# The passage from the out projection to the gate: the first products' copies placed by priority, T3's differences before the weights' sums, the norm's sums and spread behind one more product

## The chip, the cores and the metric

The kernel runs on one core of a Trainium2 chip. Its engines are TensorE (PE, with its weight loads PEld), VectorE (DVE), ScalarE (ACT), GpSimd (POOL) and SyncE (SP, which issues the DMAs). The metric is device time in microseconds; lower is better. The kernel before takes 1813.62 us, the median of three runs from 1813.46 to 1816.01.

## The reference

One layer of a hybrid decoder on 1024 tokens (and 16 meta tokens) of width 1024:

```python
h = h + jnp.concatenate([o_sb, o_ssm, o_mla], axis=-1) @ w_out[i].astype(dt)

fn = rmsnorm(h, ffn_norm_g[i])
h = h + (jax.nn.silu(fn @ w_gate[i].astype(dt)) * (fn @ w_up[i].astype(dt))) @ w_down[i].astype(dt)
```

`rmsnorm` divides each token by the root of its mean square and multiplies by a gain per channel. The three mixers (stick-breaking attention, SSD, MLA) come before, and a last norm behind. D_FF is 2816, that is 22 units of 128.

## The kernel before, in words

Everything is held with channels on the partitions: `hT[f]` is the f-th 128 channels by 1024 tokens, in two halves of 512 tokens (`HALF[c]`, c = 0 and 1). All matrix products are made in three matmuls: an operand is split into a high part (a cast, on ScalarE) and a low part (value less high part, on POOL or DVE), and high x high, low x high and high x low are summed in PSUM. `split` (L1076) is that pair: L1077 the cast, L1078 the subtraction.

The passage in question starts with the last quarter of the out projection. `last_rows(f, c)` (L1171) makes 12 matmuls (L1177 to L1179) for channel block f and half c and adds them to `hT[f]` on DVE (L1084). Half c = 0 goes into the banks named `d_ps`, half c = 1 into those named `b_ps`. When a half is complete, `squares` (L1186) stores it to DRAM, squares it on ScalarE (L1190) and adds the squares in two groups. `row_sums` (L153 on PE, L164 on DVE, the power on POOL L165; the tile is `rc`) makes each token's reciprocal root, and `row_spread` (L171 on PE) spreads it over the 128 partitions of a bank `row`. `normed` (L1117, DVE) multiplies by gain and row.

The gate and up products are made by a seven-product scheme (Strassen's) on 2 x 2 blocks: units 2p and 2p + 1 of the weights by halves of channels, against halves of channels by halves of tokens. `u11` and `u21` are the normed half c = 0 of channels 0 to 3 and 4 to 7; their split tiles are called B11 and B21 (tiles `raw`). The second half's operands are T1, T2, T3, T4 and B22, differences and sums of normed blocks. T3 is made from hT before the norm is known: ScalarE scales `hT[i]` by the gain (L1372), DVE multiplies `hT[4 + i]` by its gain and subtracts (L1374), and when the second row is there DVE multiplies the result by it (L1388). T2 = T3 + u11 (L1084) is then split into its hi and lo.

`GateUp(p)` holds one pair of units. `load` brings the weights, `sums` (L1268) makes the weights' differences and sums on DVE (four for gate, four for up; L1081 and L1084, tiles `raw` and `s2`), `split_sums` splits them. `top_first` is the first product, with B11, into two banks A (gate, up) and copies A to `r` on ScalarE (L1316); `top_second` adds the second product, with B21, to the same banks, and so can't start in a bank before it is copied. Pair p = 1 (`second`) loads its first weights early (`load_early`) and makes its `top` right behind that of p = 0; its `r` is the tile `grow`. `rest` makes the other five products; DVE adds them up (L1084, tiles `u`), with sigmoid on ScalarE (L1302) and two products on DVE (L1303, L1304). The pairs from p = 2 on follow in a loop.

What sets the order: each engine works its instructions off in the order in which they stand in its queue. A planner with a model of the engines' times places instructions where it expects them to be ready; program order is the start, `tc.high_priority(offset=n)` lets an instruction compete as if it stood n places earlier, and `tc.issue_after(ins)` keeps an instruction behind `ins` on that instruction's engine. `last_on(engine)` is the last instruction written for an engine so far.

## Time and profile before

| | us |
|---|---|
| median of 3 runs | 1813.62 |
| the profiled execution | 1819.26 |
| its span, first to last instruction | 1817.3 |
| PE busy in the span | 1722.8 (95%) |
| DVE busy | 1214.3 (67%) |
| ACT busy, POOL busy | 860.0, 858.4 (47% each) |

The last rows of the out projection run from 1055 us on, the first gate products from 1108, and the third pair of units is reached at about 1200. In a row of the timeline stand start, duration, engine, line, operation, out<-in and shape, the number of merged instructions (x4), and in brackets how long the engine was idle before and what ended that. In a row of the busy time by stretch stand the stretch, its length, the busy time of each engine with the number of instructions, the granted TensorE clock (1.00 is full), the DMA engines' share and GB/s. In the chain of waits stand start, time and engine with the tile.

### The profile page before, as it was taken

To read this page: it belongs to the slowest core of one execution; us is meant where nothing else is said; L and a number is where in the kernel's file an instruction comes from. 1 tells how busy PE (TensorE), PEld (TensorE's weight loads), DVE (VectorE), ACT (ScalarE), POOL (GpSimd) and SP (SyncE) were. 2 spreads that over 40 slices of the span, in tenths; PEclk is the share of its full clock that TensorE was granted. 3 is DMA by queue.
4 is the path that set the end of the run, shared out by engine and by line. 5 is a ranking of instruction groups with operands and counts; after the bars stand their busy time and mean duration, and the time that the engine had idled before them with its cause. 6 is when DMAs were issued, how large, how long until landed. Compare 5 with 4: busy or idle time off the path is not lost.

```text
span 1817.3 us, 26447 instructions
## 1 busy us (share of the span) xinstructions
PE 1722.8 (95%) x9769; PEld 1506.0 (83%) x9769; DVE 1214.3 (67%) x1801; ACT 860.0 (47%) x1878; POOL 858.4 (47%) x597
## 2 busy tenths in 40 slices
PE   7969999999999999999999998999999999799997
PEld 7859998999987778998888876778888888677787
DVE  8686655777544673455576558967776667899854
ACT  7545564555566646775544424422232223334333
POOL 4433334343366557563321345634333234678783
PEclk9969999999998999999999998999999999899999
DMA  4211232222443546347221342232222233733102
GB/s 157 60 53 44 78 88 73 64 70 66 116 148 106 187 159 171 103 124 263 78 88 53 108 140 102 64 99 83 80 76 81 71 98 140 286 100 95 47 1 93
DMA packets 121012, 186.93 MB, mean 103 GB/s; under 512 B 21986, under 2 KB 81412, under 8 KB 120884
## 3 DMA queue, kind: packets, MB, share of 16 engines
q1 hardware_dynamic: 101488, 169.69, 29.6%
q10 hardware_dynamic: 19396, 15.56, 2.8%
q8 instruction: 77, 1.26, 0.3%
q14 instruction: 51, 0.42, 0.1%
HBM read 131.61 MB, written 53.60 MB: 102 GB/s over the span
## 4 chain that ended last, share of the span: by engine, by line
PE 68%; DVE 17%; ACT 4%; issue 3%; DMA 3%; POOL 3%; SPq 1%; ACTq 0%; DVEq 0%; POOLq 0%
PE d_ps L142 8%; PE d_ps L143 8%; PE d_ps L144 8%; PE b_ps L1295 7%; PE b_ps L1297 7%; PE b_ps L1296 7%; DVE raw L1081 2%; PE ptg L317 2%; PE b_ps L1498 1%; PE b_ps L1497 1%; PE ptg L319 1%; PE pv L295 1%; PE b_ps L1496 1%; PE pv L296 1%; DVE hF L1084 1%
## 5 line engine op out<-in xcount | busy, mean ns | idle before, releaser
L142 PE MATMUL d_ps<-hnh,whi 128*128 128x384 f32 (+6 forms) x744 | 247.3, 333 | 1.4 <-DVE go L534 0.7
L144 PE MATMUL d_ps<-hnl,whi 128*128 128x384 f32 (+6 forms) x744 | 246.7, 332 | 0.0
L143 PE MATMUL d_ps<-hnh,wlo 128*128 128x384 f32 (+6 forms) x744 | 245.6, 330 | 0.0
L131 POOL TENSOR_TENSOR wlo<-wraw,whi 128x1024 fp32r<-128x1024 f32 (+1 forms) x57 | 135.9, 2385 | 212.0 <-ACT whi L129 203.1
L1078 POOL TENSOR_TENSOR op<-raw,op 128x512 fp32r<-128x512 f32 x83 | 125.2, 1534 | 42.1 <-ACT op L1077 38.9
L142 PEld LDWEIGHTS d_ps<-hnh,whi 128*128 128x128 f32 (+1 forms) x744 | 140.4, 189 | 5.5 <-DVE go L534 1.3
L144 PEld LDWEIGHTS d_ps<-hnl,whi 128*128 128x128 f32 (+1 forms) x744 | 140.6, 189 | 3.3 <-issue 1.0
L143 PEld LDWEIGHTS d_ps<-hnh,wlo 128*128 128x128 f32 (+1 forms) x744 | 140.4, 189 | 2.3 <-issue 0.2
L1295 PE MATMUL b_ps<-T,wh 128*128 128x512 f32 x352 | 138.4, 393 | 0.9 <-DVE u L1084 0.9
L1296 PE MATMUL b_ps<-T,wl 128*128 128x512 f32 x352 | 138.1, 392 | 0.0
L1297 PE MATMUL b_ps<-T,wh 128*128 128x512 f32 x352 | 138.0, 392 | 0.0
L303 DVE TENSOR_TENSOR pl<-ptg,ph 128x512 fp32r<-128x512 f32 (+1 forms) x160 | 99.6, 628 | 46.3 <-ACT ph L302 44.7
L1078 POOL TENSOR_TENSOR wlo<-raw,whi 128x1024 fp32r<-128x1024 f32 (+1 forms) x22 | 52.7, 2395 | 152.9 <-ACT whi L1077 152.9
L669 DVE TENSOR_TENSOR_SCAN cm<-cm,zcol 128x144 f32<-128x144 f32 (+3 forms) x64 | 103.9, 1634 | 17.8 <-ACT cm L667 17.4
L1077 ACT CAST op<-raw 128x512 fp32r<-128x512 f32 x107 | 61.4, 618 | 96.7 <-PE d_ps L1498 49.4
L302 ACT CAST ph<-ptg 128x512 fp32r<-128x512 f32 (+1 forms) x160 | 85.3, 541 | 36.3 <-PE ptg L319 24.7
L1078 POOL TENSOR_TENSOR wl<-raw,wh 128x512 fp32r<-128x512 f32 x46 | 69.8, 1526 | 58.8 <-ACT wh L1077 58.0
L1084 DVE TENSOR_TENSOR hF<-hF,b_ps 128x512 f32<-128x512 f32 (+1 forms) x96 | 59.2, 635 | 46.4 <-PE b_ps L1562 23.9
L486 DVE SCALAR_TENSOR_TENSOR cacc<-d_ps,cw,cacc 128x384 f32<-128x384 f32 (+3 forms) x108 | 61.8, 572 | 38.2 <-ACT cacc L479 36.2
L1077 ACT CAST wh<-raw 128x512 fp32r<-128x512 f32 x88 | 52.9, 616 | 67.0 <-PE b_ps L1297 64.0
L129 ACT CAST whi<-wraw 128x1024 fp32r<-128x1024 f32 (+1 forms) x57 | 58.9, 1033 | 49.4 <-PE d_ps L144 23.4
L1496 PE MATMUL b_ps<-op 128*128 128x512 f32 x183 | 72.8, 401 | 9.9 <-DVE hF L1084 6.2
(452 smaller groups left out, 5352.8 us busy)
## 6 DMA issues: line engine op xcount, KB each, us to landing
raw<-in_w_gate_dram SPq DMA_DIRECT2D x22, 512.0 KB
raw<-in_w_up_dram SPq DMA_DIRECT2D x22, 512.0 KB, 4.1
s_hid<-gs SPq DMA_DIRECT2D x44, 256.0 KB, 2.4
raw<-in_w_down_dram SPq DMA_DIRECT2D x22, 512.0 KB, 5.2
raw<-s_hid SPq DMA_DIRECT2D x22, 512.0 KB, 4.3
wraw<-in_w_o_dram SPq DMA_DIRECT2D x16, 512.0 KB, 4.0
wraw<-in_w_xbc_dram SPq DMA_DIRECT2D x12, 512.0 KB, 3.8
s_xs<-csig SPq DMA_DIRECT2D x24, 192.0 KB, 2.6
```

The lines of the kernel that those rows point to most:

```text
L131: pool.tensor_tensor(lo[:, :cols], raw[:, :cols], f32(hi[:, :cols]), op=ALU.subtract)
L142: pe.matmul(ps[:m, :n], wh, mh, start=(kt == 0), stop=False)
L143: pe.matmul(ps[:m, :n], wl, mh, start=False, stop=False)
L144: pe.matmul(ps[:m, :n], wh, ml, start=False, stop=(kt == nkt - 1))
L303: dve.tensor_tensor(pl[:, :n], pt[:, :n], f32(ph[:, :n]), op=ALU.subtract)
L669: dve.tensor_tensor_scan(rev, rev, zcol.to_broadcast([128, n_all]), 1.0, ALU.mult, ALU.add)
L1077: act.copy(hi, value)
L1078: eng.tensor_tensor(lo, value, f32(hi), op=ALU.subtract)
L1295: pe.matmul(banks[j], hi[:, ks], UH[u][k], start=start and k == 0, stop=False, skip_group_check=skip)
L1296: pe.matmul(banks[j], lo[:, ks], UH[u][k], start=False, stop=False, skip_group_check=skip)
L1297: pe.matmul(banks[j], hi[:, ks], UL[u][k], start=False, stop=stop and k == 3, skip_group_check=skip)
L1496: pe.matmul(banks[o], wh[:, os], hh, start=first, stop=False, skip_group_check=not start)
```

## The change

Four edits, all in the order of work; the operations, their shapes and their engines stay.

- The product of f = 2 for the second half is written before the sums of the first half's squares rather than behind them, those of f = 3 and 6 are kept behind the sums (before: f = 2), and f = 7 behind the spread (before: f = 3, 6, 7).
- The copies of the first products' banks on ScalarE get a priority of 2000 places.
- T3's scaling on ScalarE and its differences on DVE are written before the weights' sums, and the differences are kept behind the second half's last sum of squares (`squared`) rather than behind the second row; the weights' sums are kept behind the differences.
- The second product of the first pair is no longer cut in two (five steps behind the second half's sums, three behind its spread); all of it is kept behind the sums.

```diff
-    for f in (0, 1, 4, 5):
+    for f in (0, 1, 4, 5, 2):
         last_rows(f, 1)
     with tc.high_priority(offset=400):
         r = row_sums(acc)
...
     with tc.issue_after(summed):
-        last_rows(2, 1)
+        for f in (3, 6):
+            last_rows(f, 1)
     with tc.issue_after(rowed):
-        for f in (3, 6, 7):
-            last_rows(f, 1)
+        last_rows(7, 1)
...
-            for j in range(2):
-                act.copy(self.r[j], A[j])
+            with tc.high_priority(offset=2000):
+                for j in range(2):
+                    act.copy(self.r[j], A[j])
...
     unit.load()
-    with tc.issue_after(squared):
+    T3 = []
+    for i in range(4):
+
+        t = q_tile("T3")
+        act.activation(t, hT[i][:, HALF[1]], AF.Copy, scale=gffn[:, i : i + 1])
+        with tc.issue_after(squared):
+            dve.scalar_tensor_tensor(t, hT[4 + i][:, HALF[1]], gffn[:, 4 + i : 5 + i], t, ALU.mult, ALU.subtract)
+        T3.append(t)
+    with tc.issue_after(last_on(DVE)):
         unit.sums()
         unit.split_sums((6,))
...
-    T3 = []
-    for i in range(4):
-
-        t = q_tile("T3")
-        act.activation(t, hT[i][:, HALF[1]], AF.Copy, scale=gffn[:, i : i + 1])
-        with tc.issue_after(rowed_dve):
-            dve.scalar_tensor_tensor(t, hT[4 + i][:, HALF[1]], gffn[:, 4 + i : 5 + i], t, ALU.mult, ALU.subtract)
-        T3.append(t)
     with tc.issue_after(summed):
-        unit.top_second(slice(0, 5))
-    with tc.issue_after(rowed):
-        unit.top_second(slice(5, 8))
+        unit.top_second()
```

How this moves instructions is seen at three places. First PE, at the spread of the first row (L171, operand `rc`) among the products of the second half's rows (L1177 to L1179; the lone L153 belongs to the second half's sums). A piece of the difference, where it stood:

```order
 L1179 MATMUL b_ps<-rows,whi 128x512
-L171 MATMUL d_ps<-identr,rc 128x128 x4
-L1177 MATMUL b_ps<-raw,whi 128x512
-L1178 MATMUL b_ps<-raw,wlo 128x512
-L1179 MATMUL b_ps<-raw,whi 128x512
-L1177 MATMUL b_ps<-raw,whi 128x512
-L153 MATMUL d_ps<-ones,sq 128x1
```

It stood behind one product (f = 2) after the first half's sums. Now it stands further down:

```order
 L1178 MATMUL b_ps<-rows,wlo 128x512
 L1179 MATMUL b_ps<-rows,whi 128x512
+L171 MATMUL d_ps<-identr,rc 128x128 x4
+L153 MATMUL d_ps<-ones,sq 128x1
 L1177 MATMUL b_ps<-raw,whi 128x512
 L1178 MATMUL b_ps<-raw,wlo 128x512
```

Ahead of it, behind the sums, are now the products of f = 3 and 6; the last product, f = 7, is the only one between the spread and the first gate product. The 12 matmuls of f = 2 are spread over the places ahead of the sums, all before the last two products of the first half.

Second DVE, from the second half's last sum of squares (sq) to the sigmoid's product (L1303), where T3's differences (L1374), the weights' sums (L1081, L1084) and the second half's `rc` (L164) stand. Before:

```order
L1084 TENSOR_TENSOR sq<-sq 128x512 x2
L1081 TENSOR_TENSOR raw<-raw 128x512
L1081 TENSOR_TENSOR s_12566<-raw 128x512
L1084 TENSOR_TENSOR raw<-s_12566,raw 128x512
L1081 TENSOR_TENSOR raw<-raw,s_12566 128x512
L1081 TENSOR_TENSOR raw<-raw 128x512
L1081 TENSOR_TENSOR s_12567<-raw 128x512
L164 TENSOR_SCALAR rc<-d_ps 128x4
L1084 TENSOR_TENSOR raw<-s_12567,raw 128x512
L1081 TENSOR_TENSOR raw<-raw,s_12567 128x512
L1374 SCALAR_TENSOR_TENSOR T_12631<-hT_11268,gffn,T_12631 128x512
L1374 SCALAR_TENSOR_TENSOR T_12634<-hT_11269,gffn,T_12634 128x512
```

And in the changed kernel (the differences are now L1365):

```order
L1365 SCALAR_TENSOR_TENSOR T_12572<-hT_11270,gffn,T_12572 128x512
L1365 SCALAR_TENSOR_TENSOR T_12575<-hT_11271,gffn,T_12575 128x512
L1081 TENSOR_TENSOR raw<-raw 128x512 x2
L164 TENSOR_SCALAR rc<-d_ps 128x4
L1081 TENSOR_TENSOR s_12578<-raw 128x512
L1081 TENSOR_TENSOR s_12579<-raw 128x512
L1084 TENSOR_TENSOR raw<-s_12578,raw 128x512
L1081 TENSOR_TENSOR raw<-raw,s_12578 128x512
L1084 TENSOR_TENSOR raw<-s_12579,raw 128x512
L1081 TENSOR_TENSOR raw<-raw,s_12579 128x512
L1303 TENSOR_TENSOR gs<-b_ps,sig 128x512
```

The four differences went from behind all eight sums to ahead of them; rc had six sums ahead of it and two behind, and has the four differences and two sums ahead and six behind. The adds of hT for f = 3 and f = 6 and one sum of squares stood behind the first spread's steps (L1117) and now stand ahead of them.

Third ScalarE, at the copy of the second pair's first bank (tile `grow`) among the casts of T2. A piece of the difference:

```order
 L1302 ACTIVATE sig<-b_ps 128x512
 L1077 CAST T_12762<-T_12760 128x512
+L1317 COPY grow<-b_ps 128x512
 L1077 CAST T_12768<-T_12766 128x512
-L1316 COPY grow<-b_ps 128x512
+L1077 CAST T_12774<-T_12772 128x512
 L1077 CAST wh<-wraw 128x512 x2
 L1077 CAST wh<-raw 128x512
```

The copy moved ahead of one of the two casts that stood before it. Further up on ScalarE, T3's four scalings (L1363, before L1372) now stand ahead of the four casts of B21, which they followed.

## The prediction

> **What bounds the kernel now.** I read the page first, then the busy time by stretch, then the chain of waits and the timelines of VectorE (DVE) and TensorE (PE) over the passage.
>
> ```profile
> span 1817.3 us, 26447 instructions
> PE 1722.8 (95%) x9769; PEld 1506.0 (83%) x9769; DVE 1214.3 (67%) x1801; ACT 860.0 (47%) x1878; POOL 858.4 (47%) x597
> ...
> core 0: us, PE busy (x) PEld busy (x) DVE busy (x) ACT busy (x) POOL busy (x), PEclk, DMA share, GB/s
> 1089.50:1100.00 10.50, 8.42 (x35) 7.31 (x35) 2.10 (x5) 2.71 (x5) 4.76 (x4) 0.67 0.25 82
> 1100.00:1113.80 13.80, 13.80 (x64) 11.31 (x63) 13.33 (x17) 8.06 (x13) 8.95 (x6) 1.00 0.63 211
> 1113.80:1131.50 17.70, 11.64 (x61) 9.20 (x59) 17.53 (x24) 8.86 (x15) 8.13 (x5) 0.95 0.13 44
> 1131.50:1164.00 32.50, 30.76 (x120) 24.04 (x120) 32.50 (x37) 16.56 (x30) 25.40 (x16) 0.92 0.26 81
> 1164.00:1183.60 19.60, 18.87 (x80) 14.80 (x81) 19.56 (x28) 6.36 (x11) 6.99 (x5) 1.00 0.13 43
> 1183.60:1199.00 15.40, 12.12 (x52) 9.29 (x51) 10.31 (x10) 4.28 (x6) 8.75 (x5) 1.00 0.46 134
> 1199.00:1240.00 41.00, 41.00 (x179) 33.27 (x178) 28.24 (x34) 11.95 (x20) 15.94 (x10) 1.00 0.23 77
> ```
>
> PE is busy 95% of the span, but not here. From 1100 to 1183.6 DVE is busy 82.92 of 83.6 us (13.33 + 17.53 + 32.50 + 19.56) while PE has holes; from 1199 on PE has none. So DVE sets the pace of this passage and PE that of what follows. The chain of waits (start, us, what) says the same:
>
> ```profile
> 1099.35 0.91 PE d_ps L171 x8
> 1100.28 2.72 DVE hT L1117 x4
> ...
> 1182.99 0.61 DVE wl L1078
> 1183.62 4.82 DMA raw<-in_w_gate_dram
> ...
> 1196.77 0.47 PE b_ps L1295
> ```
>
> It leaves PE at the first spread of the norm's row (L171), runs through DVE alone to the last low part of a weight of the second unit (L1078), through the load that this frees, back through DVE, and reaches PE at 1196.77. The timeline of PE shows the waits that stand in it, and two paces:
>
> ```profile
> 1091.58 2.53 PE L153 MATMUL d_ps<-ones,sq 128*128 128x1 f32 x14 [2.55 <-DVE sq L1084]
> ...
> 1096.68 0.63 PE L1177 MATMUL b_ps<-rows,whi 128*128 128x512 f32 x1
> 1097.10 0.63 PE L1178 MATMUL b_ps<-rows,wlo 128*128 128x512 f32 x1
> ...
> 1099.19 1.05 PE L171 MATMUL d_ps<-identr,rc 128*128 128x128 f32 x8
> ...
> 1102.16 0.39 PE L1179 MATMUL b_ps<-rows,whi 128*128 128x512 f32 x1
> 1102.39 0.39 PE L1177 MATMUL b_ps<-rows,whi 128*128 128x512 f32 x1
> ...
> 1114.18 1.62 PE L153 MATMUL d_ps<-ones,sq 128*128 128x1 f32 x14
> ...
> 1120.71 1.16 PE L171 MATMUL d_ps<-identr,rc 128*128 128x128 f32 x8 [1.31 <-POOL rc L165]
> ...
> 1131.51 0.80 PE L1295 MATMUL b_ps<-raw,wh 128*128 128x512 f32 x1 [4.75 <-ACT grow L1316]
> ...
> 1192.79 0.47 PE L1295 MATMUL b_ps<-B,wh 128*128 128x512 f32 x1 [2.33 <-ACT wh L1077]
> ```
>
> Start to start a product's matmul takes 0.23 us (1102.16 to 1102.39), but 0.42 to 0.43 behind the wait of 2.55, where the granted clock of the stretch is 0.67. The wait of 4.75 for ScalarE's copy is the largest hole; it is a hole in PE, not in the chain.
>
> **The change, part by part.** The rows of DVE that it moves or meets:
>
> ```profile
> 1104.19 0.68 DVE L1084 TENSOR_TENSOR hT<-hT,b_ps 128x512 f32<-128x512 f32 x1
> ...
> 1108.53 0.69 DVE L1084 TENSOR_TENSOR sq<-sq 128x512 f32<-128x512 f32 x1
> 1109.14 1.27 DVE L1084 TENSOR_TENSOR hT<-hT,b_ps 128x512 f32<-128x512 f32 x2
> 1110.58 3.31 DVE L1084 TENSOR_TENSOR sq<-sq 128x512 f32<-128x512 f32 x2 [0.16 <-ACT sq L1190]
> ...
> 1116.53 1.80 DVE L1081 TENSOR_TENSOR raw<-raw 128x512 f32<-128x512 f32 x1
> ...
> 1118.97 0.15 DVE L164 TENSOR_SCALAR rc<-d_ps 128x4 f32<-128x4 f32 x1
> ...
> 1120.30 5.82 DVE L1374 SCALAR_TENSOR_TENSOR T<-hT,gffn,T 128x512 f32<-128x512 f32 x4
> ...
> 1126.65 2.47 DVE L1388 TENSOR_TENSOR T<-T,d_ps 128x512 f32<-128x512 f32 x4
> ```
>
> *The first spread.* Ahead of the first spread PE now has 24 more matmuls: f=2's 12 go before the sums L153, and 24 (f=3 and 6) stand between sums and spread where f=2's 12 stood. The two products in front of L153 stay the last c=0 ones, so its wait of 2.55 stays, and so does the slow stretch behind it; the 24 more therefore cost the fast pace: 24 x 0.23 = **+5.5 us**. The spread moves from 1099.19 to about 1104.7, the first norm step from 1100.28 to 1105.8. Everything of the chain stands behind that.
>
> *Work taken from behind the spread.* Three adds (hT of f=3 and f=6, one sum of squares) now run in DVE's wait before it (it sat 5 us there): 3 x 0.60, half of the 1.27 for two: **-1.8 us**. f=2's add was already ahead.
>
> *T3's differences.* Still four on the same engine; they cost 0.74 or 1.77 us each, by what POOL does meanwhile:
>
> ```profile
> L1374 DVE SCALAR_TENSOR_TENSOR T<-hT,gffn,T x4: 743/1769/1779, 1120.3 to 1124.3; 128x512 f32<-128x512 f32 x4
> ...
> 1107.37 5.97 POOL L1078 TENSOR_TENSOR raw<-hT,raw 128x512 fp32r<-128x512 f32 x4 [1.95 <-ACT raw L1077]
> ...
> 1122.13 3.45 POOL L1078 TENSOR_TENSOR wl<-wraw,wh 128x512 fp32r<-128x512 f32 x2
> ```
>
> The first of the four ran free, the rest beside POOL's splits. In the new order ScalarE scales T3 ahead of B21's casts, so POOL's four B21 splits start only when DVE comes to the differences, and all four meet them: 4 x 1.77 = 7.1 against 5.82, **+1.3** (bounds: four at 0.74, -2.9; +1.3).
>
> *The weights' sums.* Eight operations, of which one met a split (1.80 instead of 0.69). Now six stand behind rc, and the four splits of POOL that lay beside the differences (two of s2, two of wraw) come there. Four of them slowed by 1.1 each cost 4.4, less the 1.1 of before: +3.3 at most; none slowed: -1.1. The wraw splits wait for casts that come late, so I take half of the upper end, **+1.7**.
>
> *Sums of squares.* The pair at 1110.58 took 3.31 beside POOL's B21 splits; in the new order those start later and only the one beside B11's splits pays: **-1.1** (bounds -2.1, 0).
>
> By the Trainium skill, "SBUF — State Buffer", section "Who interferes with whom", an operation of VectorE with two operands in SBUF and one of GpSimd that reads SBUF shut each other out for the whole instruction. The 743 and 1769 ns agree; by the rule taken to the letter every sum that meets a split pays in full, which is the first rival's sum, not mine.
>
> *The copies on ScalarE.* ScalarE waits 7.09 us for T2's first sum and then casts it; the copy that PE waits for now passes one of the two casts:
>
> ```profile
> 1129.75 1.22 ACT L1077 CAST T<-T 128x512 fp32r<-128x512 f32 x2 [7.09 <-DVE T L1084]
> 1130.88 0.58 ACT L1316 COPY grow<-b_ps 128x512 f32<-128x512 f32 x1
> ```
>
> That is 0.6 us for PE, and nothing for the end, since DVE does not wait for PE there; were PE the bound, it would be worth these 0.6. The copy still stands behind a cast that waits for the row, so PE's hole stays.
>
> *Whole second product ahead of the second spread.* That spread passes 9 matmuls, 2.1 us of PE, hidden by a later rc: first spread +5.5, adds gone -1.8, squares -1.1, four differences now ahead of it +7.1, four sums now behind it -3.6 (3 x 0.60 and the 1.80) make +6.1 on 1118.97, so PE is through before the row can be spread, and DVE has six sums to do before it needs the row. A new short wait of PE for the low part of B11 (12 matmuls stand between spread and product where 36 stood) is off the chain too. On SP only stores of h change places with loads; the late load for the second unit still waits for POOL's last wraw split, and three splits of T2 on DVE lie between its cast and the next thing that DVE needs from ScalarE, so I take nothing for it.
>
> **Sum:** 5.5 - 1.8 + 1.3 + 1.7 - 1.1 = +5.6 us at the end of DVE's run (1183.5). The freed load, the adds behind it and PE's last wait at 1196.77 shift with it, and PE has no slack after:
>
> ```profile
> L1295 PE MATMUL b_ps<-T,wh 128*128 128x512 f32 x296 | 116.1, 392 | 0.0
> ```
>
> (the gate and up products from 1199 to 1700, idle time last). The profiled span goes from 1817.3 to 1822.9. The profiled execution took 1819.26, 5.6 more than the median 1813.62 of the runs, so I add the shift to the median: **1819.2 us**.
>
> **Rivals.** *Every meeting paid.* Sums +3.3, squares 0: 5.5 - 1.8 + 1.3 + 3.3 = +8.3, 1821.9. For it: the differences alternate with POOL strictly; against: casts hold POOL back. *The clock stays up.* The wait of 2.55 halved the pace, that of 2.33 at 1192.79 did not. If the one before L153 leaves the clock alone in the changed kernel, L153 saves 0.9 (its 14 took 1.62 at 1114.18, 2.53 here) and eleven products 0.2 each: -3.1, so +2.5, 1816.1, no change that can be told. *PE sets the pace (other side).* If DVE falls idle behind the spread by more than some 4 us in all, because its operations hardly meet POOL's, PE's holes count: 1.31 + 4.75 and the slow dozen behind the latter (12 x 0.2 = 2.4) go, about 1 comes for B11's low part: -7.5, 1806.1. For it: these holes are real; against: DVE is full for 83 us and its lower bounds sum to 5.5 - 1.8 - 2.9 - 1.1 - 2.1 = -2.4 only. That the change does not do what it says holds in part already: the copies hardly move.
>
> The Trainium skill, "TensorE: Matmul & The Clock Gate", section "Part 1: The HAM clock gate (the "warmup" mystery)", has the clock fall after an idle window of about 3.4 us that runs free of the program. By it the wait of 2.55 need not slow PE, which is the second rival; the trace shows that it did once.
>
> **How the numbers follow.** Forecast 0.48, every meeting paid 0.15, clock stays up 0.24, PE sets the pace 0.13. A measurement of this kernel can tell about 0.2%, 3.6 us. The first two are slower by more than that: 0.63; the third is within it: 0.24; the fourth faster: 0.13. The forecast's own range is 1817 to 1821.5. The range reaches up past the second case to 1822.5, and down past the third and the sum of the lower bounds (1811.2) to 1810.5.
>
> **What would show it.** Right: L171 about 5.5 us later against the c=0 rows; DVE without a hole from there to the second unit's last weight split, and that split about 5.6 later; differences at 1.77 each; PE holes as large as before. Wrong: DVE idle behind the spread, differences at 0.74, an unslowed PE behind L153, or PE holes after 1199 that take the shift up.

## The result and the profile after

The first comparison gave 1825.11 us for the changed kernel (median of 4, 1823.65 to 1828.51) beside 1814.82 for the kernel before (4, 1813.46 to 1816.89): a ratio of 1.0053, interval 1.0033 to 1.0074. The direction was forecast; the time lies above the range (1810.5 to 1822.5). Two later comparisons of the same two kernels, each with many more runs, gave less: 1.0022 (1.0011 to 1.0032) and 1.0026 (1.0014 to 1.0038), that is 4.0 and 4.7 us on 1819.37 and 1817.79.

The page of the changed kernel has the same busy engines; its span is 4.2 us longer. The busy time by stretch, in stretches that end where the same work ends as in the stretches shown of before:

```profile
span 1821.5 us, 26450 instructions
PE 1723.4 (95%) x9769; PEld 1505.3 (83%) x9769; DVE 1220.4 (67%) x1801; ACT 859.4 (47%) x1878; POOL 859.1 (47%) x597
```

```profile
1089.50:1103.20 13.70, 11.65 (x51) 9.90 (x50) 3.61 (x6) 3.86 (x7) 4.76 (x4) 0.75 0.12 48
1103.20:1118.00 14.80, 12.98 (x59) 10.46 (x58) 14.61 (x17) 9.34 (x16) 7.54 (x5) 0.88 0.49 179
1118.00:1136.00 18.00, 13.34 (x50) 9.81 (x49) 18.00 (x23) 7.49 (x13) 10.88 (x8) 0.81 0.14 44
1136.00:1169.00 33.00, 30.54 (x129) 23.78 (x128) 32.32 (x38) 15.66 (x29) 24.82 (x16) 1.00 0.24 72
1169.00:1187.20 18.20, 15.14 (x64) 11.44 (x63) 18.14 (x23) 5.68 (x10) 6.33 (x4) 1.00 0.15 48
1203.00:1240.00 37.00, 37.00 (x161) 29.98 (x161) 24.02 (x30) 11.24 (x18) 13.32 (x9) 1.00 0.27 85
```

The picture of before holds: DVE (third busy time of a row) is full from the spread to 1187.2, 83.07 of 84.0 us, and PE has holes there and none from 1203 on. The chain of waits runs the same way, from the first spread through DVE and the freed load back to PE:

```profile
1102.46 0.90 PE d_ps L171 x8
1103.39 2.72 DVE hT L1117 x4
...
1186.57 0.61 DVE wl L1078
...
1187.20 4.40 DMA raw<-in_w_gate_dram
...
1200.65 0.47 PE b_ps L1295
```

Start against start the chain seems only 3.1 to 3.9 us late. But the two executions had not reached the passage at the same time. To compare passages I take ScalarE's last cast of `ph` (L302), which lies ahead of everything the change touches, the first norm step (L1117) and DVE's row that waits for the freed load (L1081). From DVE's and ScalarE's timelines, of before and after:

```profile
1043.87 0.48 ACT L302 CAST ph<-ptg 128x384 fp32r<-128x384 f32 x1
...
1100.28 2.72 DVE L1117 SCALAR_TENSOR_TENSOR hT<-hT,gffn,d_ps 128x512 f32<-128x512 f32 x4 [0.21 <-PE d_ps L171]
...
1188.56 1.81 DVE L1081 TENSOR_TENSOR raw<-raw 128x512 f32<-128x512 f32 x1 [4.97 <-DMA raw<-in_w_gate_dram]
```

```profile
1041.98 0.48 ACT L302 CAST ph<-ptg 128x384 fp32r<-128x384 f32 x1
...
1103.39 2.72 DVE L1117 SCALAR_TENSOR_TENSOR hT<-hT,gffn,d_ps 128x512 f32<-128x512 f32 x4 [0.20 <-PE d_ps L171]
...
1191.73 2.53 DVE L1081 TENSOR_TENSOR raw<-raw 128x512 f32<-128x512 f32 x1 [4.55 <-DMA raw<-in_w_gate_dram]
```

From the start of that cast to the first norm step the kernel before takes 56.41 us and the changed one 61.41 (+5.00); from there to the load's row 88.28 and 88.34 (+0.06). Together the passage is **5.06 us longer**, and PE's restart, 1196.77 - 1043.87 = 152.90 before and 158.67 after, comes 5.8 later. The forecast for it was 5.6.

### The profile page after: what moved, and what is told of

Same layout as the page of the kernel before. It is cut to its first block, busy times and chain, and to the rows that moved or that the text cites. A ratio compares the mean times of both kernels' runs of the same rounds, so it can differ in the third digit from the quotient of the medians.

```text
span 1821.5 us, 26450 instructions
## 1 busy us (share of the span) xinstructions
PE 1723.4 (95%) x9769; PEld 1505.3 (83%) x9769; DVE 1220.4 (67%) x1801; ACT 859.4 (47%) x1878; POOL 859.1 (47%) x597
## 4 chain that ended last, share of the span: by engine, by line
PE 69%; DVE 16%; ACT 4%; issue 3%; POOL 3%; DMA 3%; SPq 1%; ACTq 0%; DVEq 0%; POOLq 0%
PE d_ps L142 8%; PE d_ps L143 8%; PE d_ps L144 8%; PE b_ps L1295 7%; PE b_ps L1296 7%; PE b_ps L1297 7%; DVE raw L1081 2%; PE ptg L317 2%; PE b_ps L1497 1%; PE b_ps L1496 1%; PE ptg L319 1%; PE b_ps L1495 1%; PE pv L296 1%; PE pv L295 1%; DVE cm L669 1%
## 5 line engine op out<-in xcount | busy, mean ns | idle before, releaser
L1078 POOL TENSOR_TENSOR op<-raw,op 128x512 fp32r<-128x512 f32 x83 | 125.5, 1538 | 42.1 <-ACT op L1077 38.9
L1296 PE MATMUL b_ps<-T,wl 128*128 128x512 f32 x352 | 138.3, 393 | 1.1 <-POOL wl L1078 1.1
L1078 POOL TENSOR_TENSOR wlo<-raw,whi 128x1024 fp32r<-128x1024 f32 (+1 forms) x22 | 52.7, 2396 | 155.4 <-ACT whi L1077 155.4
L302 ACT CAST ph<-ptg 128x512 fp32r<-128x512 f32 (+1 forms) x160 | 85.3, 541 | 36.9 <-PE ptg L319 24.4
L1078 POOL TENSOR_TENSOR wl<-raw,wh 128x512 fp32r<-128x512 f32 x46 | 69.8, 1528 | 57.3 <-ACT wh L1077 57.3
L1084 DVE TENSOR_TENSOR hF<-hF,b_ps 128x512 f32<-128x512 f32 (+1 forms) x96 | 59.1, 636 | 43.6 <-PE b_ps L1561 21.8
```

Source lines behind the costliest of these rows:

```text
L1078: eng.tensor_tensor(lo, value, f32(hi), op=ALU.subtract)
L1296: pe.matmul(banks[j], lo[:, ks], UH[u][k], start=False, stop=False, skip_group_check=skip)
```

## The experiments

In all tables below, *spread* is the time from that cast to the first norm step and *DVE* the time from there to the load's row, both as a difference to the kernel before (56.41 and 88.28 us in its profile). Each time is a ratio to runs of the kernel before on the same chip in the same comparison, with its 95% interval; each passage is read from one profile. In words, the four parts of the change are the *first rows* (f = 2 ahead of the sums, 3 and 6 ahead of the spread), *T3's place*, the *whole product*, and the *copies*.

### The two kernels once more, and the change in halves

`b_again` is the kernel before, unchanged, and `a_again` the changed one.

> The kernel before once more, timed and profiled against itself. Its first profile took 1819.26 us where its other runs took 1813.5 to 1816.9, so 10.3 us lie between the medians of before and after but only 4.2 between the two profiled spans (1817.3, 1821.5). Theory 1 (the first profile was a late one, and what made it late stands in the passage itself): a profile near 1814 shows the waits before L153 or behind it shorter or at full clock, so that the spread L171 comes some 3 us sooner than the 10.7 us that lay between the last c=0 row and L171, and the last weight split less than 83 us behind it. Theory 2 (what made it late lies elsewhere): the passage has the same length within 1 us and the 5 us are missing in another stretch. Ratio to itself 1.000 within 0.002.

> The changed kernel once more, against before: about 1.005. Its profile is compared with the first one of it: if runs of one kernel differ by several us, the two profiles should show where (a clock that falls behind the wait before L153 or does not, 3.1 us by the rows; DVE operations that meet POOL's or do not, 1.1 us each).

`spread_only` has the first rows alone:

```diff
-    for f in (0, 1, 4, 5):
+    for f in (0, 1, 4, 5, 2):
         last_rows(f, 1)
...
     with tc.issue_after(summed):
-        last_rows(2, 1)
+        for f in (3, 6):
+            last_rows(f, 1)
     with tc.issue_after(rowed):
-        for f in (3, 6, 7):
-            last_rows(f, 1)
+        last_rows(7, 1)
```

> Before, with the one edit on the rows: f=2's second-half product ahead of the first half's sums, f=3 and 6 between sums and spread, f=7 behind. My theory (the chain starts at the spread and every matmul put ahead of it costs its time): +5.5 for 24 matmuls, -1.8 for three adds of DVE, so about +3.7 us, 1.002, and this is the largest part of the change. Rival (operations of DVE that meet POOL's, brought by T3's new place, make the loss): within 1 us of before.

`spread_undone` is the changed kernel with just these lines put back.

> The changed kernel with that edit taken back, the other three kept. My theory: 3.7 us or more below the changed kernel, so about 1821 against before's 1815, L171 again where it was, and what is left is T3's place (+1.3 differences, +1.7 sums, less what the squares gain). Rival (T3's place): as slow as the changed kernel within 1 us.

| | spread, us | DVE, us | sum | time, ratio |
|---|---|---|---|---|
| kernel before again | -0.06 | +0.10 | 0.0 | 0.9999 (0.9988 to 1.0010) |
| the change again | +5.03 | +0.56 | +5.6 | 1.0022 (1.0011 to 1.0032) |
| first rows alone | +3.42 | -2.96 | +0.5 | 1.0021 (1.0011 to 1.0032) |
| all but the first rows | 0.00 | +2.31 | +2.3 | 1.0020 (1.0009 to 1.0031) |

The passage repeats to 0.1 us for the kernel before and to 0.5 for the changed one (a third profile of it, below, met another clock), while the times of single runs of the kernel before went from 1815.58 to 1824.04 in this comparison (31 runs, median 1819.37). So the passage in a profile is the finer measure here. What made the first profile of the kernel before late does not lie in it: the profile of `copies_only` below has the same order of work and 1813.79 us, and its passage is as long.

One thing has to be taken out of the passage before parts are compared: PE's clock behind the wait ahead of L153. The granted clock of the 8 us from the end of that wait is 0.57 or 0.58 in both profiles of the kernel before and both of the changed one, but 0.79 in that of the first rows alone, and its spread is 1.6 us sooner for it (+3.42 against +5.03). An estimate for the first rows alone at the clock of the others is +5.0 - 3.0 = +2.0 us: the spread comes later, and DVE takes less time behind it. My theory for this part was +3.7, its rival 0 within 1; the time, +2.0 to +5.8 us, fits the first and leaves out the second. The other parts, priced at +1.3 and +1.7, cost 2.3. By the times each half costs about as much as the whole (1.0021, 1.0020, 1.0022), so the parts do not add up there either.

### The spread sooner: the theory turned round

If the spread's place sets the end, a spread ahead of its place should gain. `spread_early` puts all of f = 2, 3, 6 and 7 behind it; `fill_f2` puts f = 2 into PE's wait of 2.55 us and nothing between sums and spread.

```diff
# spread_early
-    with tc.issue_after(summed):
-        last_rows(2, 1)
     with tc.issue_after(rowed):
-        for f in (3, 6, 7):
+        for f in (2, 3, 6, 7):
             last_rows(f, 1)
```

```diff
# fill_f2
     for f in range(KT):
         last_rows(f, 0)
+    halved = last_on(PE)
...
+    with tc.issue_after(halved), tc.high_priority(offset=400):
+        last_rows(2, 1)
+        filled = last_on(PE)
     with tc.high_priority(offset=400):
-        r = row_sums(acc)
+        with tc.issue_after(filled):
+            r = row_sums(acc)
...
-    with tc.issue_after(summed):
-        last_rows(2, 1)
```

> Kernel before, with one product moved: the rows of feature tile 2 (12 matmuls) leave from behind the row sums and stand ahead of them, directly behind the last product of the first half, where TensorE waits 2.55 us for the sum of squares; nothing is left between sums and spread. Measure: from the last inverse-transposing matmul (L997) to the first norm's spread (L171), 55.2 us in both profiles of the kernel before, and to TensorE's restart behind the last wait on the weight split, 152.8 us. Theory 1 (the passage is as long as VectorE's work from the spread on, and the spread is what sets its start): 12 matmuls at 0.23 us fill the wait, the sums end where they ended, 12 matmuls at 0.43 leave from behind them (5.1 us, of which the reciprocal root needs about 1.4 anyway): L171 at 51.5 or sooner, the restart at 148.5 to 150, time 3 to 4.5 us below the kernel before. Theory 2 (the spread's place does not set the end; the whole effect of the change sits in what follows it): L171 at 51.5, restart at 152 to 153, time within 1 us. Theory 3 (the granted clock falls behind the wait and that sets the pace): without the wait no row below 0.9 behind L153, and restart sooner by the same 3 to 4.

> Kernel before, with the rows of feature tile 2 moved behind the first spread, so that the spread stands directly behind the row sums; the wait of 2.55 us for the sum of squares stays as it is. Theory 1: L171 at 51.6 instead of 55.2 us behind the last L997 matmul, less one addition that now falls behind it (0.6 us): restart at 149.5 to 150.5, time 2 to 3.5 us below the kernel before. Theory 2: L171 at 51.6, restart unchanged at 152 to 153, time within 1 us. Theory 3: the clock falls behind the wait as before and the slow matmuls now lie behind the spread; if TensorE's pace set the end, restart at 152 to 153.

| | spread, us | DVE, us | sum | time, ratio |
|---|---|---|---|---|
| f = 2 in the wait | -2.70 | +0.16 | -2.5 | 1.0000 (0.9986 to 1.0014) |
| f = 2 behind the spread | -2.57 | +4.39 | +1.8 | 1.0022 (1.0008 to 1.0036) |

Both have the spread where it was expected, and only one keeps what it brings, in the passage; its time does not show the 2.5 us (0.9986 would be that much, the end of its interval). The rows of DVE's timeline in `spread_early` that have a wait say where the other's gain goes (the first of these waits, 0.76 for a square, stands there three times):

```profile
1112.17 0.69 DVE L1084 TENSOR_TENSOR sq<-sq 128x512 f32<-128x512 f32 x1 [0.76 <-ACT sq L1190]
...
1114.70 0.69 DVE L1081 TENSOR_TENSOR raw<-raw 128x512 f32<-128x512 f32 x1 [1.84 <-DMA raw<-in_w_gate_dram]
...
1118.43 0.80 DVE L1081 TENSOR_TENSOR raw<-raw 128x512 f32<-128x512 f32 x1 [0.92 <-DMA raw<-in_w_up_dram]
```

DVE is no longer full: it stands idle 5.0 us, first for the squares of the rows that now come behind the spread, then 2.8 us for the first weights, which land no sooner than DVE came to them before (1113.81). In `fill_f2` the wait for the weights is 1.41. So a spread ahead of its place buys only what DVE does not lose again in waits for the next things that are late.

### T3's place alone, and the copies alone

```diff
# t3_only: T3 ahead of the sums
+        with tc.issue_after(squared):
+            dve.scalar_tensor_tensor(t, hT[4 + i][:, HALF[1]], gffn[:, 4 + i : 5 + i], t, ALU.mult, ALU.subtract)
...
-    with tc.issue_after(squared):
+    with tc.issue_after(last_on(DVE)):
         unit.sums()
...
-        with tc.issue_after(rowed_dve):
-            dve.scalar_tensor_tensor(t, hT[4 + i][:, HALF[1]], gffn[:, 4 + i : 5 + i], t, ALU.mult, ALU.subtract)
```

> Kernel before, with only T3's four differences taken ahead of the weights' sums. L171 at 55.2 us as before. The changed kernel with its first products put back took 155.4 us to the restart where the kernel before takes 152.8: T3's place, the copies or the whole second product cost 2.6 us. Theory 1 (T3's place moves the sums beside GpSimd's weight splits and the splits that follow beside more of it, forecast +1.3 and +1.7 less 1.1): restart at 154.5 to 156, time +1.5 to +3. Theory 2 (it is one of the two other edits): restart at 152.5 to 153.5, time within 1 us.

`copies_only` gives the two copies of L1316 `tc.high_priority(offset=2000)` and nothing else.

> Kernel before, with only ScalarE's two copies of the first product's banks taken sooner. Theory 1 (priced at nothing: they only shorten TensorE's wait of 4.8 us, which VectorE's chain covers): TensorE's wait for the copies falls from 4.8 to 1 us, restart at 152.5 to 153.2, time within 1 us. Rival (the copies push ScalarE's casts of T or its squares back, and VectorE waits for them): the wait falls, VectorE gets an idle stretch of its own, restart at 155, time +2.5.

| | spread, us | DVE, us | sum | time, ratio |
|---|---|---|---|---|
| T3's place alone | 0.00 | -2.64 | -2.6 | 0.9994 (0.9982 to 1.0005) |
| copies alone | +0.01 | -0.09 | -0.1 | 1.0000 (0.9988 to 1.0012) |

The copies move no instruction: alone they leave the order of every engine as it was, and taken out of the changed kernel they leave its order too. So `copies_only` is a second repetition of the kernel before, and PE's wait for the copy is what it was (4.76 us). What is called the change is three parts, not four, and the copy's move past one cast, shown with the change, comes with the other parts.

T3's place, forecast as a loss, gains by itself in the passage (neither theory had that; the time, 3.3 us below to 0.9 above, can't tell it from nothing). The differences on DVE, ScalarE's work ahead of them and POOL's splits of B21, in T3's place alone (three views) and then in the changed kernel (three views):

```profile
1113.16 2.73 DVE L1364 SCALAR_TENSOR_TENSOR T<-hT,gffn,T 128x512 f32<-128x512 f32 x4
```

```profile
1106.03 2.65 ACT L1077 CAST raw<-hT 128x512 fp32r<-128x512 f32 x4 [1.07 <-DVE hT L1117]
...
1110.40 2.55 ACT L1362 ACTIVATE T<-hT,gffn 128x512 f32<-128x512 f32 x4
```

```profile
1106.72 5.97 POOL L1078 TENSOR_TENSOR raw<-hT,raw 128x512 fp32r<-128x512 f32 x4 [1.95 <-ACT raw L1077]
```

```profile
1113.40 5.83 DVE L1365 SCALAR_TENSOR_TENSOR T<-hT,gffn,T 128x512 f32<-128x512 f32 x4
```

```profile
1110.27 2.54 ACT L1363 ACTIVATE T<-hT,gffn 128x512 f32<-128x512 f32 x4
1112.72 1.65 ACT L1077 CAST raw<-hT 128x512 fp32r<-128x512 f32 x3
```

```profile
1113.40 6.98 POOL L1078 TENSOR_TENSOR raw<-hT,raw 128x512 fp32r<-128x512 f32 x4 [4.91 <-ACT raw L1077]
```

With T3's place alone ScalarE casts B21 first and scales T3 then; POOL's splits end at 1112.69, the differences start at 1113.16, and the four take 2.73 us. With the first rows too the order on ScalarE turns round: T3 is scaled first, the casts follow, and POOL's four splits start in the same moment as the four differences (both 1113.40), which take 5.83. The prediction had this turn right, but gave it to T3's place; it needs the later first rows as well (with T3's place and the whole product the four take 2.73 too, with T3's place and the first rows 5.82). By the Trainium skill, "SBUF — State Buffer", section "Who interferes with whom", such a pair of operations shuts each other out for the whole instruction; the runs agree, with 0.7 us for a difference alone and 1.8 beside POOL.

### The whole product, and the corners

```diff
# whole_only
     with tc.issue_after(summed):
-        unit.top_second(slice(0, 5))
-    with tc.issue_after(rowed):
-        unit.top_second(slice(5, 8))
+        unit.top_second()
```

> Kernel before, with only the second product whole: its last nine matmuls leave from behind the second spread and stand ahead of it. So far, from the last inverse-transposing matmul (L997) to TensorE's restart behind the last weight split, and by the shift of the rows behind it: kernel before 0, T3's place alone 2.5 us shorter, T3's place with the whole second product 2.5 us longer, the whole change 5.7 longer. Theory 1 (the whole second product, priced at nothing in the prediction, costs by itself: nine matmuls, 2.1 us, and their wait for GpSimd's weight splits stand ahead of the second spread, and VectorE waits): passage 2 to 5 us longer, time +2 to +5. Theory 2 (it costs only together with T3's new place, since only then is VectorE at the second spread so early that it waits): passage within 1 us of before, time within 1 us.

`spread_t3` is the changed kernel with these lines put back, `t3_undone` the changed kernel with T3's lines put back.

> The changed kernel with the second product cut in two again as before (its first five feature tiles ahead of the second spread, three behind it); the place of the first rows and of T3's differences stay changed. Theory 1 (the whole second product is what costs; the first rows ahead of the sums cost 0.5 to 3 us as in the run with that part alone, T3's place gives 2.5 back): passage between 2 us shorter and 0.5 us longer than the kernel before, time -2 to +0.5. Theory 2 (the later first spread costs its 5 us whenever T3's differences lie ahead of the weights' sums, as the prediction had it): passage 4 to 6 us longer, time +4 to +6.

> The changed kernel with T3's differences back behind the second spread; first rows ahead of the sums and whole second product stay. (The copies' priority stays too; alone it moves no instruction.) Passages so far against the kernel before: first rows alone +1.4 us (with the granted clock back at once behind the wait; 1.6 more where it is not), whole product alone -0.8 (clock back early as well), both with T3 +5.7. Theory 1 (what costs is the whole second product together with T3's place): passage +1 to +3, time +1 to +3. Theory 2 (what costs is the whole second product together with the later spread): passage +4 to +6, time +4 to +6.

With the runs above these are all eight corners of the three parts that do something (1 = changed):

| first rows, T3, whole | spread, us | DVE, us | sum | time, ratio |
|---|---|---|---|---|
| 0 0 0 | 0 | 0 | 0 | 1 |
| 1 0 0 | +3.42 | -2.96 | +0.5 | 1.0021 (1.0011 to 1.0032) |
| 0 1 0 | 0.00 | -2.64 | -2.6 | 0.9994 (0.9982 to 1.0005) |
| 0 0 1 | -1.59 | +1.03 | -0.6 | 1.0002 (0.9988 to 1.0017) |
| 1 1 0 | +3.42 | -2.36 | +1.1 | 1.0011 (0.9996 to 1.0026) |
| 0 1 1 | 0.00 | +2.31 | +2.3 | 1.0020 (1.0009 to 1.0031) |
| 1 0 1 | +5.01 | +1.70 | +6.7 | 1.0043 (1.0026 to 1.0059) |
| 1 1 1 | +5.00 | +0.06 | +5.1 | 1.0022 and 1.0026 |

Three readings. First, the spread has only four values: 0 and -1.6 without the first rows, +5.0 and +3.4 with them. What parts the two of a pair is the clock, not the program: in the 8 us behind the wait the granted clock is 0.57 or 0.58 in the runs at 0 and +5.0 and 0.79 in those at -1.6 and +3.4, and the changed kernel itself gave both (below). At one clock the sums of 1 0 0, 0 0 1 and 1 1 0 are 1.6 us more, so +2.0, +1.0 and +2.6.

Second, DVE's stretch does not add up: the three single parts sum to -4.6, together they give +0.1. The whole product, priced at nothing, makes it longer at every corner: +1.0 alone, +4.9 on T3's place, +4.7 on the first rows, +2.4 on both (two profiles of one kernel differ by up to 0.8 here, so the 1.0 is little). Theory 1 of `whole_only` expected 2 to 5 us from it alone and Theory 2 none without T3's place; the first fell, and the second misses the corner with the first rows, where Theory 2 of `t3_undone` (+4 to +6) came nearest. `spread_t3` lies between its two theories.

Third, the places where the parts meet show when the stretch is cut in three: from the first norm step to T3's product with the second row (L1388 in the kernel before), from there to the second half's first norm step (L1117), and from there to the load's row. In the middle piece lie T2's sums and their four low parts (L1078, tile `T`). Differences to the kernel before, us:

| first rows, T3, whole | to T3's product | T2 | behind it |
|---|---|---|---|
| 1 0 0 | -1.3 | -2.7 | +1.0 |
| 0 1 0 | -2.7 | -1.3 | +1.4 |
| 0 0 1 | +0.8 | -0.5 | +0.8 |
| 1 1 0 | -1.4 | -2.7 | +1.7 |
| 0 1 1 | -2.7 | +3.6 | +1.4 |
| 1 0 1 | -0.8 | +1.1 | +1.3 |
| 1 1 1 | -0.8 | -2.2 | +3.0 |

On T3's place or on the first rows alone, the whole product pays in T2's piece: 4.9 of its 4.9 us and 3.8 of its 4.7. On T3's place it pays as waits of DVE for ScalarE that T3's place alone does not have (that one waits 0.15 us there). DVE's rows, and those of ScalarE ahead of them:

```profile
1132.86 0.69 DVE L1078 TENSOR_TENSOR T<-T,T 128x512 fp32r<-128x512 f32 x1 [2.02 <-ACT T L1077]
1134.93 5.00 DVE L1078 TENSOR_TENSOR T<-T,T 128x512 fp32r<-128x512 f32 x3 [1.39 <-ACT T L1077]
```

```profile
1131.72 0.59 ACT L1317 COPY grow<-b_ps 128x512 f32<-128x512 f32 x1 [7.92 <-PE b_ps L1297]
1132.20 0.62 ACT L1077 CAST T<-T 128x512 fp32r<-128x512 f32 x1
```

ScalarE stands 7.92 us at the copy of the second pair's bank, until PE has made it, and T2's first cast stands behind the copy; with T3's place alone two of T2's casts stand ahead of it. At the corner with the first rows and the whole product DVE has no wait at all there, but the four low parts take 6.88 us, where with the first rows alone they take 2.48. First rows alone, then both:

```profile
1136.49 2.48 DVE L1078 TENSOR_TENSOR T<-T,T 128x512 fp32r<-128x512 f32 x4
```

```profile
1131.22 6.88 DVE L1078 TENSOR_TENSOR T<-T,T 128x512 fp32r<-128x512 f32 x4
```

POOL's splits of weights lie beside them in both, and with the first rows alone it is POOL that pays: two of its splits take 5.34 us there and 3.41 at the other corner. Why the one engine pays in the one run and the other in the other, and where the +3.0 in the changed kernel's last piece comes from, was not settled.

### A version that gains, and the change a third time

`fill_t3` joins the two parts that shorten the passage: f = 2's rows in PE's wait (`fill_f2`) and T3's place (`t3_only`); `early_t3` joins T3's place with `spread_early`. `fill_t3_f3` is `fill_t3` with f = 3's rows between sums and spread. The diffs are those above, joined.

> Kernel before, with feature tile 2's rows in TensorE's wait ahead of the row sums (first spread 2.7 us sooner in the run with that alone, passage 2.5 shorter, VectorE 1.4 us idle until the first weights have landed) and T3's four differences ahead of the weights' sums (alone: passage 2.5 shorter). Theory 1 (VectorE's chain carries the passage; T3's differences also cover the wait for the weights): the two add up, passage 4 to 6 us shorter, time 4 to 6 us below the kernel before. Theory 2 (something else sets the end once 2.5 us are gone, TensorE or the loads of the weights): passage 2 to 3 us shorter, time -2 to -3.

> Kernel before, with feature tile 2's rows behind the first spread (that alone: first spread 2.6 us sooner, yet the passage 1.8 to 2.4 us longer, VectorE idle 5.0 us in it, of which 2.8 on the first weights' loads and 2.3 on squares) and T3's four differences ahead of the weights' sums. Theory 1 (VectorE's idle time for the loads is filled by T3's differences): passage 1.5 to 4 us shorter than the kernel before, time -1.5 to -4. Theory 2 (the passage grew because of what meets GpSimd's splits, not because of the idle time): passage 0 to 2.5 us longer, time 0 to +2.5.

> The version with feature tile 2's rows in TensorE's wait ahead of the row sums, nothing between sums and spread, and T3's differences ahead of the weights' sums, unchanged. If the 4.5 us were real: ratio 0.9965 to 0.9985 of the kernel before, first spread 51.5 us behind the last L997 matmul, passage 3 us shorter. If they were spread between runs: ratio above 0.999.

> The same with feature tile 3's rows (12 matmuls, 2.8 us) between sums and first spread, where TensorE waits 2.2 us for the reciprocal root. Theory 1 (VectorE's start sets the passage): the spread 0.6 us later, passage 0.5 to 1 us longer than without, time the same or up to 1 us above it. Theory 2 (TensorE sets the passage now): 12 matmuls leave from behind the spread, passage 1.5 to 2.2 us shorter, time 1.5 to 2 us below it.

> The changed kernel as it is. Theory 1 (the passage's growth is the whole effect, the forecast's base was too low): passage 5.5 to 5.9 us longer than before's, time 3 to 6 us above the runs of the kernel before that share this call. Theory 2 (there is a loss outside the passage, as the first comparison's 10 us would have it): time 8 to 12 us above them.

| | spread, us | DVE, us | sum | time, ratio |
|---|---|---|---|---|
| f = 2 in the wait, T3 early | -2.62 | -0.53 | -3.2 | 0.9975 (0.9963 to 0.9987) |
| the same again | -2.74 | -1.25 | -4.0 | 0.9989 (0.9975 to 1.0004) |
| the same, f = 3 before the spread | -3.09 | +0.28 | -2.8 | 0.9983 (0.9968 to 0.9998) |
| f = 2 behind the spread, T3 early | -2.62 | +0.87 | -1.8 | 0.9992 (0.9980 to 1.0004) |
| the change a third time | +3.42 | -0.24 | +3.2 | 1.0026 (1.0014 to 1.0038) |

PE's timeline of `fill_t3` shows no wait ahead of the sums; what is left is a wait for the root:

```profile
1089.41 1.84 PE L153 MATMUL d_ps<-ones,sq 128*128 128x1 f32 x16
1093.45 2.06 PE L171 MATMUL d_ps<-identr,rc 128*128 128x128 f32 x8 [2.20 <-POOL rc L165]
```

T3's differences take the time in which `fill_f2` waited 1.41 us for the weights, as expected; the two gains do not add up in full (-2.5 and -2.6 give -3.2 and -4.0, between the two theories). Against the kernel before the gain is clear of noise the first time and not when repeated; against the changed kernel the repetition is enough (0.9975 to 1.0004 there, 1.0014 to 1.0038 for the changed kernel beside it). With f = 2 behind the spread T3's place turns +1.8 into -1.8, but the time is not clear of noise.

With f = 3 between sums and spread the passage is no shorter, so PE does not set it. The spread was expected 0.6 us later and came 0.4 to 0.5 sooner: the wait for the root is gone, and the eight matmuls of the spread take 1.05 us where behind that wait they take 2.06 and 1.94.

## Why the prediction was right and wrong

**The base was too low; the shift was about right.** The step that failed is "so I add the shift to the median". The sum was +5.6 us, and the passage grew by 5.1, 5.6 and 3.2 us in three profiles (PE's restart by 5.8 in the first). But 1813.62 was the median of three runs that lay low: the kernel before has medians of 1819.37, 1816.98, 1820.23 and 1817.79 in the four later comparisons (31, 35, 35 and 27 runs, together 1811.4 to 1824.6). These four were on four chips, and the chip of the three runs is not known, so the share of the chip in these levels stays open. The profiled execution's 1819.26 stood on the page and was nearer the middle than the three; I set it aside. From those four medians the forecast's +5.6 gives 1822.6 to 1825.8, and the changed kernel's medians are 1825.11, 1822.64 and 1821.96. The shift in time was 4.0 and 4.7 us in the two large comparisons, with intervals (2.0 to 5.8 and 2.5 to 6.9) that hold 5.6.

The first comparison's 10.3 us between medians does not fit as well. Its interval, 1.0033 to 1.0074, begins where that of the second ends (1.0032), so two sets of four runs being a low and a high draw is a likely account and not a shown one. A loss outside the passage, the other account, was tested by the third comparison and is not needed there: it would have shown 8 to 12 us, and 4.2 lie between the medians.

**The first spread: right, a little too dear.** Forecast +5.5; measured +5.0 where the clock behaved as in the profile of before (granted clock 0.57 over the 8 us behind the wait). The wait ahead of L153 did not stay at 2.55; it is 2.05 in each profile with the first rows:

```profile
1091.92 2.54 PE L153 MATMUL d_ps<-ones,sq 128*128 128x1 f32 x14 [2.05 <-DVE sq L1084]
```

**"The clock stays up" happened in part.** Busy time and granted clock of PE in three-microsecond stretches behind that wait, in the profile after and in the third repetition of the same kernel, counted from the same point:

```profile
1092.00:1095.00 3.00, 3.00 (x16) 0.60 0.01 3
1095.00:1098.00 3.00, 3.00 (x9) 0.50 0.00 0
1098.00:1101.00 3.00, 3.00 (x12) 0.76 0.00 0
```

```profile
1094.20:1097.20 3.00, 3.00 (x18) 0.80 0.01 2
1097.20:1100.20 3.00, 3.00 (x10) 0.63 0.00 0
1100.20:1103.20 3.00, 3.00 (x16) 1.00 0.22 87
```

The clock falls in both, and in the second it falls later and is back sooner; the spread is 1.6 us earlier for it (+3.42 against +5.00). The rival had -3.1 and a chance of 0.24; half of that is what comes, with the change and also without it (-1.59 in `whole_only`, where the order up to the first spread is that of before). By the Trainium skill, "TensorE: Matmul & The Clock Gate", section "Part 1: The HAM clock gate (the "warmup" mystery)", the window of about 3.4 us that decides runs free of the program: that one program meets two lengths of slow stretch agrees, that a wait of 2.05 us with matmuls of one column behind it is enough does not.

**DVE's stretch: the sum came out right by luck.** -1.8 + 1.3 + 1.7 - 1.1 = +0.1 was forecast, and +0.06, +0.56 and -0.24 measured. Where the three pieces of the stretch begin, and T2's low parts, before and after:

```profile
1132.04 5.75 DVE L1078 TENSOR_TENSOR T<-T,T 128x512 fp32r<-128x512 f32 x4
1137.72 2.71 DVE L1117 SCALAR_TENSOR_TENSOR hT<-hT,gffn,d_ps 128x512 f32<-128x512 f32 x4
```

```profile
1128.95 2.47 DVE L1387 TENSOR_TENSOR T<-T,d_ps 128x512 f32<-128x512 f32 x4
...
1134.34 1.89 DVE L1078 TENSOR_TENSOR T<-T,T 128x512 fp32r<-128x512 f32 x3
1136.91 1.03 DVE L1078 TENSOR_TENSOR T<-T,T 128x512 fp32r<-128x512 f32 x1 [0.68 <-ACT T L1077]
1137.86 2.71 DVE L1117 SCALAR_TENSOR_TENSOR hT<-hT,gffn,d_ps 128x512 f32<-128x512 f32 x4
```

All terms of the sum lie in the first piece, which ends with T3's product (1126.65 before, 1128.95 after); it is 0.8 us shorter. Adds and squares, three of six gone, gave -3.4 (-2.9 forecast). The four differences cost as much as before (5.82 and 5.83 us, not the 7.1 behind the +1.3), since the first of the four still ran free. The eight sums with `rc` took 2.7 more (1113.81 to 1120.30 before, 1119.15 to 1128.35 after; +1.7 forecast). What stands behind was left out of the sum: T2's piece is 2.2 us shorter, since its four low parts no longer take 5.75 us, and the rest up to the load's row is 3.0 longer (3.5 and 1.6 in the other two profiles). These two, never priced, and the misses of the first piece made +0.06.

The prices of single parts do not hold either. T3's place, +3.0 with the weights' sums, is -2.64 alone; the whole product, 0, is up to +4.9 beside another part. The reason given for that 0, that PE is through before the row can be spread, holds: PE waits 0.43 us for POOL's root at the second spread. The cost came by ways that were not looked at, the queue of ScalarE and T2's low parts beside POOL. The last weight split came 5.5 us later from the cast (1186.57 - 1041.98 = 144.59 against 1182.99 - 1043.87 = 139.12), 5.6 forecast.

**The rest.** No hole in DVE was forecast, and the profile has one of 0.68 us. PE's hole of 4.75 in the profile of before is now 3.42 for the low part of a weight (L1296 on POOL) and 0.81 for the copy; the "new short wait for the low part of B11" is there, 1.82 us:

```profile
1109.10 0.50 PE L1297 MATMUL b_ps<-raw,whi 128*128 128x512 f32 x1 [1.82 <-DVE raw L1078]
...
1127.93 0.79 PE L1296 MATMUL b_ps<-raw,wl 128*128 128x512 f32 x1 [3.42 <-POOL wl L1078]
...
1133.81 0.50 PE L1295 MATMUL b_ps<-raw,wh 128*128 128x512 f32 x1 [0.81 <-ACT grow L1317]
```

"PE sets the pace" fell: T3's place alone, with DVE 2.6 us shorter, brings the end of the passage 2.6 sooner, and twelve matmuls taken from behind the spread (`fill_t3_f3`) make it no shorter. "Every meeting paid" (+8.3) fell too; +6.7 was reached only at the corner without T3's place. That the copies do nothing was named in passing and holds entirely.

## What to carry to other kernels

When runs of one kernel spread over more than the effect, a few of them are no base: measure between two events in the trace that enclose the change, from an event ahead of it, and state the forecast as a difference. Parts of a change that meet on one full engine do not add up: price each with the others taken out and put in, above all where an engine ahead (here ScalarE) may turn its order round. If a term for "moves nothing the end waits for" is zero, name the queue in which it now stands ahead of something. And when two profiles are compared, look at the granted clock first: here it alone was worth 1.6 us, as much as a part of the change.

## What the hardware showed that was not expected

The same order of instructions on every engine, run three times, comes to the same point up to 6.2 us apart: ScalarE's last `ph` cast at 1043.87 in the profile of before, at 1044.63 in `b_again` and at

```profile
1038.40 0.48 ACT L302 CAST ph<-ptg 128x384 fp32r<-128x384 f32 x1
```

in `copies_only`. The mean granted clock of the whole span is higher there: 0.979 in `copies_only` (span 1811.9 us), 0.972 and 0.971 in the other two (1817.3 and 1818.6). A part of it arises at 275 to 315 us, where PE's granted clock dips in the one (before, the first of the two views) and not in the other:

```profile
275.00:295.00 20.00, 17.88 (x94) 0.96 0.33 86
295.00:315.00 20.00, 20.00 (x126) 0.95 0.18 60
```

```profile
275.00:295.00 20.00, 18.99 (x104) 1.00 0.35 86
295.00:315.00 20.00, 20.00 (x131) 1.00 0.21 67
```

At 275 us both had made 1612 matmuls; after these 40 us PE is 15 matmuls further on in the second. Whether a short wait is followed by a slow stretch, and by how long a one, varies from run to run. PE's wait for a weight's cast near the end of the passage shows it too: behind 2.33 us at 1192.79 the granted clock of the next 5 us is 1.00 in the profile of before, behind 2.42 us at the same place in `b_again` it is 0.66. That such stretches make all of the spread between runs, 8 us and more, was not shown.
